# A conditioned short-convolution layer on one core: idle products in fewer instructions, adaLN's later pieces spread anew among the first weight loads, and first loads and splits in a fixed order

## The chip, the cores and the metric

The kernel runs on one core of a Trainium2 chip. The metric is device time in microseconds, the median of several runs; beside it stands one execution taken by the hardware profiler. The engines are TensorE (PE, its weight loads PEld), VectorE (DVE), ScalarE (ACT), GpSimd (POOL) and SyncE (SP), which issues nearly all DMAs. Each engine runs its instructions in the order in which the built program has them.

## What is computed

One layer: RMS norm, adaLN modulation by a conditioning vector, a gated short convolution, a gated residual, and a last RMS norm. T = 256 tokens, D = 2048, E = 4096, all in float32.

```
h = rmsnorm(x, norm_g)
shift, scale, gate = split(silu(c) @ ada_w + ada_b, 3)      # ada_w is 2048 x 6144
h = h * (1 + scale) + shift
b_gate, c_gate, v, g = split(h @ w_in, 4)                   # w_in is 2048 x 16384, 128 MB
u = causal_depthwise_conv(c_gate * v, conv_w)               # 3 taps
y = b_gate * u * silu(g)
x = x + gate * (y @ w_out)                                  # w_out is 4096 x 2048, 32 MB
return rmsnorm(x, final_g)
```

## The kernel before

**Products.** Features lie along partitions, tokens along the free axis; `hT` holds the modulated activations of 16 feature blocks k (0 to 15). To keep float32's accuracy each weight block is split into `hi`, a cast to fp32r by ACT (L338), and `lo`, the rest, by DVE (L339), and so is `hT`. Each block of 128x128 weights gives three products of 256 columns (L469): hi by hi, hi by lo, lo by hi.

**Two ways through w_in.** The products with a block k of `hT` can only be made when adaLN's shift and scale for k are known. `ada_w`'s columns for the first two k come first and on the path (16 rows of blocks `first_ada`, L211 to L219, summed by DVE at L365 and in part on PE by `sum0`). The others come in seven groups of two k, each in eight *pieces* of two DMAs of 256 KB (`ada_piece`, L425; tile `at`, four buffers) and two sums on DVE of each piece (L448, L450). Behind the last piece of a group four transposes on PE (`tp_g`, L457) and ACT, DVE give shift and scale. While these arrive, the first half of w_in's columns (four chunks `ch` of 512 columns in each of four quarters `q`) is worked in *passes*: `parts(chs, q, k0, k1, ...)` (L507) takes two chunks over the k at hand in one PSUM bank each (tile `mm_s`, three buffers), and its result goes to `acc` in SBUF: `keep` copies it out by ACT (L501) or adds it by DVE (L503). A later pass is opened either by ACT, which copies `acc` back into the bank (a seed, L517), or is added afterwards. The second half of the columns (tile `mm_b`) comes behind it with all k at once, and then the products with w_out (`mm_o`).

**The plan.** `plan()` (L55) works out with rough costs which pass covers which k, which pieces stand behind which load (`between`), and which passes are seeded. Credit grows by 1.5 a load of 1 MB, and each whole unit gives out one piece.

**Order.** The start, up to L404, is pinned in the order of the code. Behind that a scheduler orders each engine's instructions by data, buffers and priorities; adaLN's sums have a lower priority (`later(GIVE)`). `behind(ended)` holds the first loads, splits and sums behind the pinned part, but leaves their order among themselves to the scheduler.

**Names used below.** *Load n* is the n-th `raw_s` load of `parts` (L531; load 1 has 0.5 MB, the others 1 MB, three buffers). *Pieces p0 to p7* are the first group (k 2 and 3), p8 opens the next. *Chunk b0* is the bank that is filled from `raw0`, b1 that of load 1; load n from 2 on feeds b(2n-2) and b(2n-1). In the first passes a chunk is 24 products. With three banks, chunk b(n) needs the bank of b(n-3) copied out.

**Idle products.** `idle(n, where)` (L252) makes products of ones in the start, where PE would have nothing to do. Nothing reads them.

Of the kernel before, what the change touches and what calls it, by code (L numbers as in the profile page):

```python
# [49 lines left out]


SHARE = 1.5


def plan():  # L55
    steps, ready = [], [0.0] * ADA[0]
    done = {}
    pieces = [(sum(ADA[:g]), nk, i) for g, nk in enumerate(ADA) if g for i in range(4 * nk)]
    load, pe, dve, act = 0.0, 4.0, 0.0, 0.0
    burst = SLOT // P  # L60
    credit = -1.5

    def ada():
        nonlocal load, dve
        piece = pieces.pop(0)
        load = max(load, dve - AAHEAD) + ALOAD
        dve = max(dve, load + 2.0) + VPIECE
        if piece[2] == 4 * piece[1] - 1:
            ready.extend([dve + ALAG] * piece[1])
        return piece  # L70

    def products(n, need):

        nonlocal load, pe, dve, act, credit
        between = []
        load = max(load, pe - WAHEAD)
        pe = max(pe, need, load + min(n, burst) * LOAD + WLAG) + n * PRODUCTS
        for s0 in range(0, n, burst):
            sn = min(burst, n - s0)
            load += sn * LOAD  # L80
            act = max(act, load + 2.0) + sn * SBLOCK
            dve = max(dve, load + 2.0) + sn * VBLOCK
            credit += SHARE * sn / burst
            between.append([])
            while pieces and credit >= 1.0:
                credit -= 1.0
                between[-1].append(ada())
        return between

    order = [((ch, ch + 1), q) for ch in range(0, NCH, 2) for q in QUARTERS]  # L90
    new = [((0,), QUARTERS[0]), ((1,), QUARTERS[0])] + order[1:]
    while new or any(k < KT for k in done.values()):
        before = []
        hi = sum(r <= pe for r in ready)
        if new:
            p = new.pop(0)
            k0 = done[p] = 0
            if p not in order:
                del done[p]
                done[order[0]] = hi  # L100
        else:
            old = [p for p in order if done[p] < KT]
            p = old[0] if hi == KT else min(old, key=lambda p: done[p])
            k0 = done[p]
            while hi == k0:
                while len(ready) == hi:
                    before.append(ada())
                    credit -= 1.0
                pe = max(pe, ready[hi])
# [12 lines left out]
        steps.append((before, *p, k0, hi, hows, between))  # L122
        if p in order:
            done[p] = hi
    return steps


@with_exitstack
def short_conv_layer(ctx: ExitStack, tc: tile.TileContext, x, c, norm_g, ada_w, ada_b, w_in, conv_w, w_out, final_g, out):
    nc = tc.nc  # L130
# [22 lines left out]
    after = mybir.DependencyInfo(mybir.DependencyClass.NoSync, mybir.DependencyReason.DATA)  # L153
# [12 lines left out]
        ended.update(last)  # L166

    @contextmanager
    def behind(last):

        traced = nc.cur_bb.bb.instructions
        n = len(traced)
        yield
        for ins in list(traced[n:]):
            if ins.engine in last:
                tc.add_manual_dep(ins, last[ins.engine], after, reason="behind")

    @contextmanager
    def later(n):
# [10 lines left out]
    ended = {}  # L190
# [5 lines left out]
    rows2 = const.tile([96, P], F32, tag="rows2", name="rows2")  # L196
    HX = D // 2
    GIVE = 300
    IDLE = (20, 8, 20, 4, 4, 5, 11, 4)
    xt = [[slot([P, HX], f"x{t}{dh}") for dh in range(2)] for t in range(TT)]  # L200
    for t in range(TT):
        for dh in range(2):
# [8 lines left out]
    for n in range(KT // 4):  # L211
        at = wpool.tile([P, SLOT], F32, tag=("lo", "hi")[n % 2], name="at0", bufs=3)
        at = at.rearrange("p (k s f) -> p k s f", k=4, s=2)
        if n == 0:
            wpool.tile([P, 32], F32, tag="line3", name="line3", bufs=1)
        for j, kk in ((0, 2), (2, 2)) if n < 3 else ((0, 2), (2, 1), (3, 1)):
            for s in range(2):
                nc.sync.dma_start(at[:, j : j + kk, s, :], adas[:, 4 * n + j : 4 * n + j + kk, s, 0 : NK0 * P])
        first_ada.extend(at[:, i] for i in range(4))  # L219
# [31 lines left out]

    def idle(n, where):  # L252
        for _ in range(IDLE[n]):
            nc.tensor.matmul(where[:, 0, :], ones_r[:, 0:P], ones_r[:, T:], start=True, stop=True, skip_group_check=True)

    warm = const.tile([P, 1], F32, tag="warm", name="warm")
    silu = nc.scalar.activation(silu_c, turn(rows1, 64, 80, None), AF.Silu)
# [138 lines left out]
    w = CT * P  # L396
# [28 lines left out]
    def ada_piece(k0, nk, piece):  # L425
        w = nk * P
        kk = ASLOT // (2 * w)
        if piece == 0:
            sums[k0] = adap.tile([P, 2, 2 * P], F32, tag="gv", name="gv")
        gv = sums[k0][:, :, 0:w]  # L430
        j = piece * kk
        at = adap.tile([P, ASLOT], F32, tag="at", name="at", bufs=4)
        at4 = at.rearrange("p (k s f) -> p k s f", k=kk, s=2)
        for s in range(2):
            with behind(ended if first_loads else {}):
                nc.sync.dma_start(at4[:, :, s, :], adas[:, j : j + kk, s, k0 * P : k0 * P + w])
            first_loads[:] = first_loads[1:]
        with later(GIVE):
            ada_sums(j, kk, at4, gv)
        if j + kk == KT:  # L440
            ada_done(k0, nk, gv)

    def ada_sums(j, kk, at4, gv):
        for i in range(kk):
            c_k = silu_c[:, j + i : j + i + 1]
            if j + i == 0:
                with behind(ended):
                    nc.vector.tensor_scalar_mul(gv, at4[:, i], c_k)  # L448
            else:
                nc.vector.scalar_tensor_tensor(out=gv, in0=at4[:, i], scalar=c_k, in1=gv, op0=ALU.mult, op1=ALU.add)  # L450

    def ada_done(k0, nk, gv):

# [6 lines left out]
        modulate(k0, nk, (gs[:, 0:nk], gs[:, nk : 2 * nk]))  # L460

    opener = [None]
    first_loads = [None] * 16

    def product(dst, hi, lo, k, i, begins, left, ends):

# [35 lines left out]
        else:  # L502
            nc.vector.tensor_tensor(out=acc[ch, q], in0=bank, in1=acc[ch, q], op=ALU.add)  # L503

    first_pieces = [None] * 3

    def parts(chs, q, k0, k1, seeds, between):  # L507

# [17 lines left out]
        for s0, some in zip(range(k0, k1, step), between):  # L526
            sk = min(step, k1 - s0)
            n = sk * w
            raw = raw_tile("raw_s")
            with behind(ended if first_loads else {}):  # L530
                nc.sync.dma_start(  # L531
                    raw[:, :n].rearrange("p (k f) -> p k f", k=sk),
                    w_in[0, s0 * P : (s0 + sk) * P, col : col + w].rearrange("(k p) f -> p k f", p=P),
                )
            first_loads[:] = first_loads[1:]
            with behind(ended if first_pieces else {}):
                hi, lo = split(raw, n)
            first_pieces[:] = first_pieces[1:]
            for piece in some:
                ada_piece(*piece)  # L540
            for j, (bank, seed) in enumerate(zip(banks, seeds)):
# [241 lines left out]
```

## Time and profile before

| | |
|---|---|
| median of 3 runs | 918.99 us (917.21 to 919.25) |
| the profiled execution | 923.62 us, span 921.8 us |
| PE busy | 901.1 us, 98% |
| DVE, ACT busy | 626.7 us (68%), 467.0 us (51%) |
| mean granted clock of PE | 0.995 |
| DMA | 227.64 MB, mean 247 GB/s |

The span is the time from the first to the last instruction; the profiled execution's own time holds a little around it. A row of the timeline has the start and the length in us from the span's start, engine, line, operation and operands (written tile, arrow, read tiles), the count of merged instructions, and in brackets the idle time before it and who ended it. A list of waits has the total in us, how often, and the longest. `SPq` is SP's queue of DMA issues. The granted clock is PE's, 1.00 the full one.

### The profile page before, as it was taken

The page shows a single profiled execution, that of the slowest core. Times are in us where ns is not written, and L with a number is a line of the kernel's source. Part 1 is how long each engine was busy: PE and PEld are TensorE (multiplying, and loading weights), DVE is VectorE, ACT ScalarE, POOL GpSimd, SP SyncE. Part 2 cuts the span into 40 slices and gives each one's busy share as a digit, 9 for nine tenths or more (in the row PEclk, how much of TensorE's full clock was granted, in tenths as well). Part 3 has the DMA queues.
Part 4 walks back from the last instruction along what each step waited for, and adds up shares of the span by engine and source line. Part 5 has one row for each costly group of instructions (what it writes and reads, how often), then busy time and mean ns, then how long its engine had stood idle before and what let it go on. Part 6 is the DMA issues. An engine that isn't in the chain of part 4 may idle for free.

```text
span 921.8 us, 16333 instructions
## 1 busy us (share of the span) xinstructions
PE 901.1 (98%) x7091; PEld 867.5 (94%) x7091; DVE 626.7 (68%) x600; ACT 467.0 (51%) x445; POOL 2.3 (0%) x9
## 2 busy tenths in 40 slices
PE   7899999999999998999999999999999999999996
PEld 7899999999999998999999999999999988888885
DVE  5699998988887879976554554445554545545882
ACT  6579877656544648454334333443344433444333
POOL 1000000000000000000000000000000000000000
PEclk9999999999999999999999999999999999999999
DMA  9999999999888577777666665666666486566542
GB/s 305 373 362 362 331 376 367 338 339 357 306 302 319 184 254 278 240 227 223 191 185 196 200 197 183 193 201 202 183 185 197 140 347 228 187 202 204 184 137 91
DMA packets 146775, 227.64 MB, mean 247 GB/s; under 512 B 5456, under 2 KB 103808, under 8 KB 146320
## 3 DMA queue, kind: packets, MB, share of 16 engines
q1 hardware_dynamic: 146576, 226.51, 73.3%
q8 instruction: 55, 0.90, 0.4%
q14 instruction: 16, 0.13, 0.0%
q0 software_dynamic: 96, 0.08, 0.0%
q10 hardware_dynamic: 32, 0.01, 0.0%
HBM read 224.49 MB, written 2.10 MB: 246 GB/s over the span
## 4 chain that ended last, share of the span: by engine, by line
PE 83%; DMA 7%; DVE 5%; ACT 2%; issue 1%; SPq 0%; ACTq 0%; DVEq 0%
PE mm_b L469 38%; PE mm_s L469 26%; PE mm_o L681 6%; PE mm_o L680 6%; PE mm_o L679 6%; DMA at_g<-in_ada_w_dram 3%; DMA at<-in_ada_w_dram 2%; DVE lo L339 2%; DMA raw_s<-in_sc_w_in_dram 1%; DVE gacc L611 1%; ACT hi L338 1%; DMA x<-in_x_dram 1%; ACT mm_s L517 0%; ACT acc L501 0%; DVE acc L413 0%
## 5 line engine op out<-in xcount | busy, mean ns | idle before, releaser
L469 PE MATMUL mm_b<-hT,hi 128*128 128x256 f32 x2048 | 348.4, 276 | 0.0
L469 PE MATMUL mm_s<-hT,hi 128*128 128x256 f32 x2048 | 340.4, 278 | 6.4 <-ACT acc L501 3.1
L469 PEld LDWEIGHTS mm_s<-hT,hi 128*128 128x128 f32 x2048 | 302.0, 189 | 7.7 <-ACT acc L501 3.3
L469 PEld LDWEIGHTS mm_b<-hT,hi 128*128 128x128 f32 x2048 | 308.5, 188 | 0.0
L469 PE MATMUL mm_b<-hT,lo 128*128 128x256 f32 x1024 | 282.6, 276 | 0.0
L469 PE MATMUL mm_s<-hT,lo 128*128 128x256 f32 x1024 | 266.2, 278 | 0.9 <-DVE lo L339 0.8
L339 DVE TENSOR_TENSOR lo<-raw,hi 128x2048 fp32r<-128x2048 f32 x64 | 146.7, 2292 | 128.9 <-ACT hi L338 128.9
L338 ACT CAST hi<-raw 128x2048 fp32r<-128x2048 f32 x64 | 122.5, 1913 | 202.1 <-PE mm_b L469 150.8
L469 PEld LDWEIGHTS mm_b<-hT,lo 128*128 128x128 f32 x1024 | 192.2, 188 | 0.1
L469 PEld LDWEIGHTS mm_s<-hT,lo 128*128 128x128 f32 x1024 | 185.2, 189 | 1.5 <-DVE lo L339 1.5
L338 ACT CAST hi<-raw_s 128x2048 fp32r<-128x2048 f32 (+1 forms) x64 | 121.4, 1898 | 83.2 <-PE mm_s L469 69.2
L339 DVE TENSOR_TENSOR lo<-raw_s,hi 128x2048 fp32r<-128x2048 f32 (+1 forms) x64 | 145.5, 2273 | 22.5 <-ACT hi L338 19.0
L339 DVE TENSOR_TENSOR lo<-raw_o,hi 128x2048 fp32r<-128x2048 f32 x32 | 73.3, 2291 | 65.5 <-ACT hi L338 65.4
L338 ACT CAST hi<-raw_o 128x2048 fp32r<-128x2048 f32 x32 | 61.0, 1907 | 106.8 <-PE mm_o L681 84.0
L680 PE MATMUL mm_o<-lo,y 128*128 128x512 f32 x256 | 99.3, 389 | 0.0
L681 PE MATMUL mm_o<-hi,y 128*128 128x512 f32 x256 | 99.3, 389 | 0.0
L679 PE MATMUL mm_o<-hi,y 128*128 128x512 f32 x256 | 99.3, 389 | 0.0
L450 DVE SCALAR_TENSOR_TENSOR gv<-at,silu_c,gv 128x512 f32<-128x512 f32 x105 | 78.6, 749 | 2.6 <-DMA at<-in_ada_w_dram 0.8
L680 PEld LDWEIGHTS mm_o<-lo,y 128*128 128x128 f32 x256 | 48.0, 188 | 10.0
L679 PEld LDWEIGHTS mm_o<-hi,y 128*128 128x128 f32 x256 | 48.0, 188 | 10.0
L681 PEld LDWEIGHTS mm_o<-hi,y 128*128 128x128 f32 x256 | 48.0, 188 | 9.9
L501 ACT COPY acc<-mm_s 128x1024 f32<-128x1024 f32 x50 | 50.3, 1013 | 12.4 <-PE mm_s L469 12.4
(109 smaller groups left out, 388.4 us busy)
## 6 DMA issues: line engine op xcount, KB each, us to landing
raw<-in_sc_w_in_dram SPq DMA_DIRECT2D x64, 1024.0 KB, 5.6
raw_s<-in_sc_w_in_dram SPq DMA_DIRECT2D x63, 1024.0 KB, 7.4
raw_o<-in_sc_w_out_dram SPq DMA_DIRECT2D x32, 1024.0 KB, 5.2
at<-in_ada_w_dram SPq DMA_DIRECT2D x126, 256.0 KB, 7.3
at_g<-in_ada_w_dram SPq DMA_DIRECT2D x32, 512.0 KB, 7.3
x<-in_x_dram SPq DMA_DIRECT2D x4, 512.0 KB, 6.6
big<-in_x_dram SPq DMA_DIRECT2D x2, 1024.0 KB, 8.6
out_dram<-big SPq DMA_DIRECT2D x4, 512.0 KB, 2.9
```

What stands on the lines that cost most here:

```text
L338: nc.scalar.copy(hi[:, :n], raw[:, :n])
L339: nc.vector.tensor_tensor(out=lo[:, :n], in0=raw[:, :n], in1=hi[:, :n].bitcast(F32), op=ALU.subtract)
L450: nc.vector.scalar_tensor_tensor(out=gv, in0=at4[:, i], scalar=c_k, in1=gv, op0=ALU.mult, op1=ALU.add)
L469: mm = last_mm[0] = nc.tensor.matmul(dst, w, h[:, k], start=begins and left, stop=ends, skip_group_check=True)
L501: nc.scalar.copy(acc[ch, q], bank)
L611: nc.vector.scalar_tensor_tensor(out=ga, in0=at3[:, i, :], scalar=s, in1=ga, op0=ALU.mult, op1=ALU.add)
L679: nc.tensor.matmul(po, yh, hi[:, o], start=opens, stop=False, skip_group_check=True)
L680: nc.tensor.matmul(po, yh, lo[:, o], start=False, stop=False, skip_group_check=True)
L681: nc.tensor.matmul(po, yl, hi[:, o], start=False, stop=ct == NCT - 1, skip_group_check=True)
```

## The change

The kernel's products, results and sizes stay, apart from the idle products. Five edits go together:

1. The idle products come in fewer and wider instructions: 512 columns instead of 256, and for `idle(0)` to `idle(2)` in plain FP32 instead of fp32r (their ones read through `bitcast`).
2. The last four of the first adaLN columns come in eight single DMAs of 128 KB instead of two of 256 KB and four of 128.
3. `credit` starts at 0.0 and no longer at -1.5, by which `plan` hands out pieces one or two loads earlier, and comes to other passes from the ninth on. Behind it a list `PACE` spreads the pieces of the first ten loads anew: none behind the first three, then 2, 1, 2, 2, 2, 2, 2.
4. The first 28 DMAs of `parts` and `ada_piece` go through `load`, which holds each behind the one before on SP, in the order of the code.
5. The first ten splits are held in order on ACT and DVE (`advance=True`), and the sums of pieces behind the last split that the code has ahead of them.

```diff
+PACE = (0, 0, 0, 2, 1, 2, 2, 2, 2, 2)
...
-    credit = -1.5
+    credit = 0.0
...
+    blocks = [b for step in steps for b in step[-1]][: len(PACE)]
+    some = [piece for b in blocks for piece in b]
+    for b, n in zip(blocks, PACE):
+        b[:], some = some[:n], some[n:]
+    blocks[-1].extend(some)
     return steps
...
-    def behind(last):
+    def behind(last, advance=False):
...
+        if advance:
+            last.update((ins.engine, ins.name) for ins in list(traced[n:]) if ins.engine in last)
...
-    IDLE = (20, 8, 20, 4, 4, 5, 11, 4)
+    IDLE = (2, 1, 3, 2, 2, 3, 5, 2)
...
-        for j, kk in ((0, 2), (2, 2)) if n < 3 else ((0, 2), (2, 1), (3, 1)):
+        for j, kk in ((0, 2), (2, 2)) if n < 3 else ((0, 1), (1, 1), (2, 1), (3, 1)):
...
         for _ in range(IDLE[n]):
-            nc.tensor.matmul(where[:, 0, :], ones_r[:, 0:P], ones_r[:, T:], start=True, stop=True, skip_group_check=True)
+            both = ones_r.bitcast(F32) if n < 3 else ones_r
+            nc.tensor.matmul(where[:, 0:2, :], both[:, 0:P], both, start=True, stop=True, skip_group_check=True)
...
         for s in range(2):
-            with behind(ended if first_loads else {}):
-                nc.sync.dma_start(at4[:, :, s, :], adas[:, j : j + kk, s, k0 * P : k0 * P + w])
-            first_loads[:] = first_loads[1:]
+            load(at4[:, :, s, :], adas[:, j : j + kk, s, k0 * P : k0 * P + w])
...
-            if j + i == 0:
-                with behind(ended):
+            with behind(ended if first_pieces or j + i == 0 else {}):
+                if j + i == 0:
                     nc.vector.tensor_scalar_mul(gv, at4[:, i], c_k)
-            else:
-                nc.vector.scalar_tensor_tensor(out=gv, in0=at4[:, i], scalar=c_k, in1=gv, op0=ALU.mult, op1=ALU.add)
+                else:
+                    nc.vector.scalar_tensor_tensor(out=gv, in0=at4[:, i], scalar=c_k, in1=gv, op0=ALU.mult, op1=ALU.add)
...
-    first_loads = [None] * 16
+    first_loads = [None] * 28
+
+    def load(dst, src):
+
+        ins = nc.sync.dma_start(dst, src)
+        if first_loads:
+            sp = ins.ins.engine
+            tc.add_manual_dep(ins.ins, ended[sp], after, reason="in order")
+            ended[sp] = ins.ins.name
+            first_loads.pop()
...
-    first_pieces = [None] * 3
+    first_pieces = [None] * 10
...
-            with behind(ended if first_loads else {}):
-                nc.sync.dma_start(
...
-            first_loads[:] = first_loads[1:]
-            with behind(ended if first_pieces else {}):
+            load(
+                raw[:, :n].rearrange("p (k f) -> p k f", k=sk),
+                w_in[0, s0 * P : (s0 + sk) * P, col : col + w].rearrange("(k p) f -> p k f", p=P),
+            )
+            with behind(ended if first_pieces else {}, advance=True):
                 hi, lo = split(raw, n)
-            first_pieces[:] = first_pieces[1:]
+            del first_pieces[:1]
```

SP's DMAs behind the first two w_in loads, before. `raw_s_401` is load 2, `raw_s_467` load 3, `raw_s_537` load 4, `raw_s_602` load 5, `raw_s_672` load 6; `at_408`, `at_473`, `at_478`, `at_543`, `at_608` are p0 to p4.

```order
L531 DMA raw_s_401<-in_sc_w_in_dram 128x2x1024
L436 DMA at_408<-in_ada_w_dram 128x2x256 x2
L531 DMA raw_s_467<-in_sc_w_in_dram 128x2x1024
L436 DMA at_473<-in_ada_w_dram 128x2x256 x2
L436 DMA at_478<-in_ada_w_dram 128x2x256 x2
L436 DMA at_543<-in_ada_w_dram 128x2x256 x2
L531 DMA raw_s_537<-in_sc_w_in_dram 128x2x1024
L531 DMA raw_s_602<-in_sc_w_in_dram 128x2x1024
L436 DMA at_608<-in_ada_w_dram 128x2x256 x2
L531 DMA raw_s_672<-in_sc_w_in_dram 128x2x1024
```

The same place after: loads 2 to 6 are `raw_s_347`, `407`, `478`, `543`, `613`, and p0 to p4 `at_414`, `419`, `484`, `549`, `554`.

```order
L474 DMA raw_s_347<-in_sc_w_in_dram 128x2x1024
L474 DMA raw_s_407<-in_sc_w_in_dram 128x2x1024
L474 DMA at_414<-in_ada_w_dram 128x2x256 x2
L474 DMA at_419<-in_ada_w_dram 128x2x256 x2
L474 DMA raw_s_478<-in_sc_w_in_dram 128x2x1024
L474 DMA at_484<-in_ada_w_dram 128x2x256 x2
L474 DMA raw_s_543<-in_sc_w_in_dram 128x2x1024
L474 DMA at_549<-in_ada_w_dram 128x2x256 x2
L474 DMA at_554<-in_ada_w_dram 128x2x256 x2
L474 DMA raw_s_613<-in_sc_w_in_dram 128x2x1024
```

Load 3 moved ahead of p0, load 4 ahead of p2 and p3, and p3 and p4 now both stand ahead of load 6, where before load 6 stood behind p4 alone.

DVE at loads 4 to 6, before: `lo_540` is the low part of load 4, `lo_605` of load 5, `lo_675` of load 6; `gv_407` is the running sum of the first group.

```order
L450 SCALAR_TENSOR_TENSOR gv_407<-at_473,silu_c_133,gv_407 128x512
L339 TENSOR_TENSOR lo_540<-raw_s_537,hi_539 128x2048
L450 SCALAR_TENSOR_TENSOR gv_407<-at_478,silu_c_133,gv_407 128x512
L339 TENSOR_TENSOR lo_605<-raw_s_602,hi_604 128x2048
L450 SCALAR_TENSOR_TENSOR gv_407<-at_478,silu_c_133,gv_407 128x512
L450 SCALAR_TENSOR_TENSOR gv_407<-at_543,silu_c_133,gv_407 128x512 x2
L339 TENSOR_TENSOR lo_675<-raw_s_672,hi_674 128x2048
```

And after, where `lo_481` is the low part of load 4, `lo_546` of load 5, `lo_616` of load 6:

```order
L455 TENSOR_SCALAR gv_413<-at_414,silu_c_135 128x512
L348 TENSOR_TENSOR lo_481<-raw_s_478,hi_480 128x2048
L457 SCALAR_TENSOR_TENSOR gv_413<-at_414,silu_c_135,gv_413 128x512
L457 SCALAR_TENSOR_TENSOR gv_413<-at_419,silu_c_135,gv_413 128x512 x2
L348 TENSOR_TENSOR lo_546<-raw_s_543,hi_545 128x2048
L457 SCALAR_TENSOR_TENSOR gv_413<-at_484,silu_c_135,gv_413 128x512 x2
L457 SCALAR_TENSOR_TENSOR gv_413<-at_549,silu_c_135,gv_413 128x512 x2
L457 SCALAR_TENSOR_TENSOR gv_413<-at_554,silu_c_135,gv_413 128x512
L348 TENSOR_TENSOR lo_616<-raw_s_613,hi_615 128x2048
```

The second sum of p0 (`at_414`), which frees its buffer, moved behind the low part of load 4; before, p1's second sum (`at_473`, the first row there) stood ahead of that already.

ACT at the same place: the order of casts and copies is the same up to the copy-out of b2 (`acc02`) behind the cast of load 4; b3's copy-out (`acc12`) moved ahead of the cast of load 5. The last passes over the first half of w_in, as `plan` gives them (chunks, quarter, k from and to, loads), are before

```
(0,1) q0 10-16: 3   (2,3) q1 12-16: 2   (2,3) q2 14-16: 1   (2,3) q3 14-16: 1   (2,3) q0 6-16: 5
```

and after

```
(0,1) q0 14-16: 1   (2,3) q1 14-16: 1   (2,3) q2 6-16: 5   (2,3) q3 8-16: 4   (2,3) q0 12-16: 2
```

Behind the pass with q0 of channels 0 and 1 stands their mixing (`mixed`, L552: products, convolution and splits on DVE and ACT).

More of the change, by code (lines that the diff above doesn't have):

```diff
@@ L529, in parts @@
             raw = raw_tile("raw_s")
-            with behind(ended if first_loads else {}):
[L531 to L534, printed above, removed]
-            first_loads[:] = first_loads[1:]
-            with behind(ended if first_pieces else {}):
+            load(
[3 more added lines that the diff above has]
+            with behind(ended if first_pieces else {}, advance=True):
                 hi, lo = split(raw, n)
-            first_pieces[:] = first_pieces[1:]
+            del first_pieces[:1]
             for piece in some:
```

## The prediction

> **What bounds the kernel now.** I read the busy times by stage first, to see where TensorE (PE) waits at all; then the list of waits, for what ends these waits; then the timeline of the first 50 us. In the stage table the first pair of a row after the length is PE's busy time with its instructions.
>
> ```profile
> core 0: us, PE busy (x) PEld busy (x) DVE busy (x) ACT busy (x) POOL busy (x), PEclk, DMA share, GB/s
> 0.00:26.00 26.00, 19.76 (x142) 18.69 (x143) 13.73 (x26) 16.77 (x28) 2.33 (x9) 0.98 0.95 309
> 26.00:49.00 23.00, 19.94 (x151) 19.74 (x150) 16.18 (x17) 14.85 (x13) 0.00 (x0) 0.87 1.02 366
> 49.00:300.00 251.00, 250.57 (x2205) 250.14 (x2205) 223.22 (x250) 168.60 (x185) 0.00 (x0) 1.00 0.98 342
> 300.00:385.00 85.00, 81.17 (x701) 79.87 (x700) 75.91 (x91) 52.18 (x55) 0.00 (x0) 1.00 0.69 235
> 385.00:733.00 348.00, 348.00 (x3071) 347.90 (x3070) 192.41 (x148) 144.17 (x109) 0.00 (x0) 1.00 0.63 196
> 733.00:908.00 175.00, 175.00 (x804) 146.05 (x804) 102.67 (x66) 64.54 (x46) 0.00 (x0) 1.00 0.58 200
> ```
>
> PE is the bound, and the change leaves its products alone. From 385 to 908 us it never waits, and nothing there changes. What can be won lies in four stages: 6.24 us idle before 26, 3.06 in 26 to 49, 0.43 in 49 to 300, 3.83 in 300 to 385.
>
> ```profile
> PE mm_s L469 <- ACT acc L501: 3.1, 1, 3.1
> PE mm_s L469 <- DVE acc L503: 2.4, 1, 2.4
> PE mm_s L469 <- ACT mm_s L517: 0.9, 2, 0.5
> PE mm_s L469 <- DVE lo L339: 0.8, 2, 0.5
> ```
>
> The 3.1 us is one wait, and the timeline shows what stands behind it:
>
> ```profile
> 28.26 1.22 DVE L339 TENSOR_TENSOR lo<-raw_s,hi 128x1024 fp32r<-128x1024 f32 x1
> 31.19 3.15 SPq L531 DMA_DIRECT2D raw_s<-in_sc_w_in_dram  x2
> 31.65 2.29 DVE L339 TENSOR_TENSOR lo<-raw_s,hi 128x2048 fp32r<-128x2048 f32 x1
> 40.07 1.07 PE L469 MATMUL mm_s<-hT,lo 128*128 128x256 f32 x8
> 41.34 1.90 ACT L338 CAST hi<-raw_s 128x2048 fp32r<-128x2048 f32 x1 [4.70 <-DMA raw_s<-in_sc_w_in_dram]
> 43.14 1.01 ACT L501 COPY acc<-mm_s 128x1024 f32<-128x1024 f32 x1
> 44.20 2.61 PE L469 MATMUL mm_s<-hT,hi 128*128 128x256 f32 x16 [3.06 <-ACT acc L501]
> ```
>
> ScalarE (ACT) runs in order. The copy-out of bank b2 (43.14) could have run at 36, but it stands behind the cast of load 4, which waits 4.70 us for its data. PE's next chunk, b5, takes b2's bank. So a late load 4, needed by PE only at b6, stops PE at b5. The chain gives that load as
>
> ```profile
> 31.19 10.07 DMA raw_s<-in_sc_w_in_dram
> ```
>
> It was issued at 31.19 and landed at 41.26, behind the pieces p0 to p3 of adaLN (eight loads of 256 KB) in a busy queue. And the wait costs more than itself:
>
> ```profile
> 45.00:46.00 1.00, 1.00 (x10) 1.00 (x9) 1.00 (x2) 1.00 (x2) 0.00 (x0) 0.83 1.02 351
> 46.00:47.00 1.00, 1.00 (x6) 1.00 (x6) 1.00 (x2) 1.00 (x2) 0.00 (x0) 0.50 0.88 230
> 47.00:48.00 1.00, 1.00 (x7) 1.00 (x6) 1.00 (x1) 0.81 (x2) 0.00 (x0) 0.50 0.87 226
> 48.00:49.00 1.00, 1.00 (x7) 1.00 (x7) 1.00 (x2) 1.00 (x1) 0.00 (x0) 0.50 0.99 400
> 49.00:50.00 1.00, 1.00 (x10) 1.00 (x10) 0.93 (x3) 1.00 (x2) 0.00 (x0) 0.96 1.13 406
> ```
>
> The granted clock (first number after POOL) is halved from 45.9 to 49.3: 0.17+0.50+0.50+0.50+0.04 = 1.71 us of PE time lost. Together 4.77 us hang on load 4.
>
> **Part by part.** *Loads in fixed order.* On SP load 3 now stands ahead of p0, and only p0 and p1 stand ahead of load 4: four loads of 256 KB less.
>
> ```profile
> 17.00:18.00 1.00, 1.00 (x11) 1.00 (x11) 0.96 (x2) 1.00 (x3) 0.00 (x0) 1.00 1.10 349
> 35.00:36.00 1.00, 1.00 (x12) 1.00 (x11) 0.64 (x1) 1.00 (x2) 0.00 (x0) 1.00 1.11 377
> ```
>
> At 349 to 377 GB/s these 1.05 MB take 2.8 to 3.0 us. Load 4 lands at 41.26 - 2.9 = 38.4, if it is issued in time: its buffer is load 1's, free at 28.26+1.22 = 29.5, and its queue is then still full, so bandwidth decides. Cast 1.90, copy 1.01 with the same small steps (41.26 to 44.20 is 2.94): b5 can start at 41.35. PE ends b4 at 40.07+1.07 = 41.14, so 0.2 us remain of 3.06, too little to be read as idle by the clock. This gives -2.85 -1.71 = -4.55 us.
>
> *The price: p4 stands ahead of load 6.* `at` has four buffers, so p4 waits until both sums of p0 are done; p0's second sum now stands on VectorE (DVE) behind the low part of load 4. SP waits with everything behind p4. Chunks and loads there:
>
> ```profile
> 59.57 1.98 PE L469 MATMUL mm_s<-hT,hi 128*128 128x256 f32 x16
> 62.29 1.98 PE L469 MATMUL mm_s<-hT,hi 128*128 128x256 f32 x16
> 22.50 0.98 SPq L436 DMA_DIRECT2D at<-in_ada_w_dram  x2
> 33.86 0.74 DVE L450 SCALAR_TENSOR_TENSOR gv<-at,silu_c,gv 128x512 f32<-128x512 f32 x1
> raw<-in_sc_w_in_dram SPq DMA_DIRECT2D x64, 1024.0 KB, 5.6
> raw_s<-in_sc_w_in_dram SPq DMA_DIRECT2D x63, 1024.0 KB, 7.4
> ```
>
> Load 4's cast ends at 40.4, its low part at 42.7 (2.29), the sum at 43.4; p4's two loads 0.98, so load 6 is issued at 44.4 into a queue that has run empty. I take the 5.6 us of the last row but one (that queue is the less filled), not 7.4: landed 50.0, cast to 52.0, b6's bank copied out to 53.0. PE, a chunk every 2.72 us, wants that bank for b9 at 41.35+4x2.72 = 52.2: 0.8 us of new wait. With 7.4 it is 2.6, with less than 4.8 nothing. By the Trainium skill, "DMA: Bandwidth & Descriptors", section "Anatomy of one DMA", a DMA costs 2.0 us and its bytes at 436 GB/s; by that estimate load 6 takes 4.4 us, and the sum below would be 0.8 us better. The trace has no such load under 5.0 us, so I keep the rows.
>
> On DVE five sums (3.75) follow the low parts of loads 5 and 6; behind 52.0 that is low part 6 to 54.3, sums to 58.0, low part 7 to 60.3, three sums to 62.3, when p7 is complete. PE reaches the transposes of p7's result (`tp_g`, in chunk b12) at 53.0+3x2.72+0.9 = 62.1: 0.2 us. Behind that I take nothing: the stage table has PE waiting 0.43 us in the 251 from 49 on, and the loads behind load 7 are the same bytes in nearly the same order.
>
> *Eight single loads of 128 KB at the end of the first adaLN columns.* The chain into the first product is last landing, last sum, sum0, features:
>
> ```profile
> at<-in_ada_w_dram SPq DMA_DIRECT2D x1, 128.0 KB, 4.9
> 15.41 3.34 SPq L218 DMA_DIRECT2D at<-in_ada_w_dram  x5
> 23.48 0.75 DVE L365 SCALAR_TENSOR_TENSOR gv<-at,silu_c,gv 128x512 f32<-128x512 f32 x1 [0.41 <-DMA at<-in_ada_w_dram]
> 24.29 1.08 PE L351 MATMUL sum<-ones,gv 128*128 128x1 f32 x8 [0.41 <-DVE gv L365]
> ```
>
> SP's issues are 0.75 us apart here whatever their size (five in 3.34), since each waits for the landing of the eighth DMA before it. Two DMAs more put the last one's issue 1.5 us later. If its 4.9 us to landing is a latency, the first product is 1.5 late; if it is bandwidth (DMA share 1.10 in the row of 17 us, and the bytes are the same), nothing. I take 0.3, near the second end, for the queue and so for load 4 too.
>
> *Idle products.* In columns streamed, `idle(0..2)` pass 20, 8, 20 x 256 now; after, 2, 1, 3 x 512 in plain FP32, and the rest keep 1024, 1024, 1536, 2560, 1024 against 1024, 1024, 1280, 2816, 1024.
>
> ```profile
> 4.24 4.35 PE L254 MATMUL tp_x<-ones_r 128*128 128x256 f32 x20
> ```
>
> No FP32 product of that width is in the trace. At the rate of the others, 512 columns take 0.43 us cold (4.35/20x2), so `idle(0)` is over at 5.1; at four times that, 3.5 us, at 7.7. Neither end moves the first product, which waits for DMA until 24.29; but a colder PE could. I take nothing: a clock of 0.87 over 26 to 49 means 3.0 us lost, 1.3 more than the stretch above, so the first products run at half clock already; and b5 waits for load 4, not for them. The bound is +0.8 if the clock is lost for another 1.7 us of products ahead of b4's end.
>
> *The plan.* `credit` starts at 0 and no longer at -1.5, so passes move: one pass of columns 2 and 3 now takes k 0 to 4, the short passes of one load at the end stand elsewhere, and 15 adds of 1.22 us lie on DVE (12 before), with 27 instead of 34 seeding copies on ACT. PE's products stay. In 49 to 300 the table has DVE at 223 of 251 us: 3.7 more are covered. In 300 to 385 (75.9 of 85) they are not safely so:
>
> ```profile
> 339.35 0.75 DVE L611 SCALAR_TENSOR_TENSOR gacc<-at_g,silu_c,gacc 128x512 f32<-128x512 f32 x1 [5.64 <-DMA at_g<-in_ada_w_dram]
> 352.90 2.29 DVE L339 TENSOR_TENSOR lo<-raw_s,hi 128x2048 fp32r<-128x2048 f32 x1
> 356.37 1.22 DVE L503 TENSOR_TENSOR acc<-mm_s,acc 128x1024 f32<-128x1024 f32 x1
> ```
>
> DVE waits 5.64 us for a gate load, falls behind, and the add that frees a bank is late: the 2.4 us wait. Before, three passes of together four loads follow the mixing of channels 0 and 1 (the last two of one load each); after, one of one load and then one of five. The ends are -3.8 (all waits of this stage go) and +3.8 (they double). I take 0.
>
> Sum: -4.55 + 0.8 + 0.2 + 0.3 + 0 = -3.25 us. The profiled execution took 923.62 us (span 921.8), so 920.4 of its kind; the median of the runs shown is 918.99, 4.6 below it, and I carry the difference over: 915.7.
>
> **Rivals.** (1) *The wait only moves to load 6.* For it: SP is one queue, and p4 stands in it ahead of load 6. If load 6 takes the 10 us that load 4 took, it lands at 54.4, b9 waits 5.2 us and the clock falls again: -4.55+5.2+1.7+0.5 = +2.9, slower (921.9). It decides from a landing of 8.9 us on (7.2 if the clock falls as well); at 7.4 with the clock kept it gives 917.5. Against it: that queue has run empty.
> (2) *The late stage gets worse.* Place: DVE from 300 us; mechanism: an add behind mixing and gate sums, which wait for a landing. From +3.3 us there on the gain is gone; doubled waits give 919.5, three times the waits 923.3. For it: three adds more, and one-load passes still there. Against: PE's longest pass follows at once.
> (3) *The late stage gets better.* Its 3.8 us vanish: 911.9.
> (4) *The clock term isn't there.* The Trainium skill, "TensorE: Matmul & The Clock Gate", section "Part 1: The HAM clock gate", lets the clock fall after an idle window of about 3.4 us that runs freely. The row has a fall after only 3.06 us idle, so the trace does not bear that out as a rule for whole windows; but a fall lasts 3.4 us here too, and where its edges lie may differ from run to run. Where timed runs before the change kept the clock, the gain is 3.25-1.71 = 1.5: 917.5.
> (5) *The reorder does nothing*, as load 4 is late for another reason (its issue): then the 0.8, 0.2 and 0.3 stay: 920.3 at most, 919 if they hide in the old wait.
>
> **Numbers.** My forecast (-3.25, all within -1.9 to -5): 0.52. Rival 1: slower 0.04, half way 0.06. Rival 2: 0.10, half of it past the old time. Rival 3: 0.10. Rival 4: 0.10. Rival 5: 0.08. A change under 0.2% (1.8 us) can't be told from none in this kernel, so 917.15 to 920.8 is "the same". Faster: 0.52 + 0.10 + a third of rivals 1's half way and 4 (0.05) = 0.67. Slower: 0.04 + 0.05 + 0.01 = 0.10. The same: the rest, 0.23. The range runs from rival 3 (911.9) to the point where half of rival 2 and all of the slower ones are left out: 912 to 919.5. My forecast's own range is 914 to 917.1.
>
> **What would show it.** Right: no wait of PE over 1 us before 100 us; load 4's cast begins at 38 to 39, and the granted clock stays whole from 29 us on. Load 6's cast begins near 50, with a wait of under 1 us at the chunk b9. The first product starts at 26.2 to 26.6. PE's idle in 300 to 385, about 3.8. Wrong: the cast of load 4 still near 41; a wait of 3 us or more at b9 or at `tp_g`; a second half-clock stretch; a first product past 27; or more than 7 us idle behind 300.

## The result, and the profile after

The changed kernel is slower: 927.20 us median of six runs (926.47 to 930.7), against 919.52 us for the kernel before on the same chip (917.21 to 920.75). The ratio is 1.0093, 95% interval 1.0072 to 1.0113. The profiled execution took 930.7 us (span 928.6), against 923.62 (span 921.8).

The stage table of the changed kernel, its stages cut where its own work ends (columns as before):

```profile
core 0: us, PE busy (x) PEld busy (x) DVE busy (x) ACT busy (x) POOL busy (x), PEclk, DMA share, GB/s
26.00:49.00 23.00, 20.97 (x178) 20.23 (x177) 15.73 (x15) 14.42 (x12) 0.00 (x0) 1.00 0.90 309
49.00:60.00 11.00, 8.03 (x71) 7.83 (x70) 7.20 (x9) 4.72 (x4) 0.00 (x0) 1.00 0.89 315
60.00:90.00 30.00, 25.68 (x201) 25.11 (x201) 24.85 (x30) 19.31 (x24) 0.00 (x0) 0.89 1.02 367
90.00:120.00 30.00, 28.40 (x248) 28.00 (x247) 27.59 (x33) 26.31 (x31) 0.00 (x0) 1.00 1.01 345
120.00:300.00 180.00, 180.00 (x1589) 180.00 (x1588) 160.06 (x177) 100.54 (x112) 0.00 (x0) 1.00 0.95 333
300.00:392.00 92.00, 89.81 (x773) 89.30 (x773) 86.74 (x103) 56.77 (x58) 0.00 (x0) 0.98 0.76 260
```

The stretch from 26 to 49 us is better than it was: 2.0 us idle instead of 3.1, and the clock whole instead of 0.87. The loss stands where the prediction had put 1 us: 3.0 us idle in 49 to 60, and 4.3 us idle with a clock of 0.89 in 60 to 90. Another 1.6 us stand in 90 to 120; the late stage has 2.2 instead of 3.8. The list of waits names them:

```profile
PE mm_s L485 <- ACT acc L517: 4.2, 2, 3.0
PE mm_s L485 <- DVE hT L341: 2.8, 1, 2.8
PE mm_s L485 <- DVE acc L519: 2.2, 1, 2.2
PE mm_s L485 <- ACT mm_s L533: 1.5, 1, 1.5
PE mm_s L485 <- ACT hT L339: 1.5, 1, 1.5
```

(Lines of the changed kernel: L347 is the cast, L348 the low part, L455 and L457 the sums, L464 the transposes `tp_g`, L466 their reads, L339 to L341 the features, L474 every load, L485 the products, L517 and L519 copy-out and add, L533 the seed.)

The first wait of 3.0 us is that of load 6, in rows of the timeline from SP, DVE, ACT and PE (39.18 is the cast of load 4, 42.05 the first products of b5):

```profile
35.09 9.90 SPq L474 DMA_DIRECT2D at<-in_ada_w_dram  x4
39.18 1.91 ACT L347 CAST hi<-raw_s 128x2048 fp32r<-128x2048 f32 x1 [2.71 <-DMA raw_s<-in_sc_w_in_dram]
41.12 2.29 DVE L348 TENSOR_TENSOR lo<-raw_s,hi 128x2048 fp32r<-128x2048 f32 x1 [2.84 <-ACT hi L347]
42.05 2.10 PE L485 MATMUL mm_s<-hT,hi 128*128 128x256 f32 x16 [1.22 <-ACT acc L517]
43.33 2.32 DVE L457 SCALAR_TENSOR_TENSOR gv<-at,silu_c,gv 128x512 f32<-128x512 f32 x3
45.09 0.41 SPq L474 DMA_DIRECT2D raw_s<-in_sc_w_in_dram  x1
45.68 4.74 SPq L474 DMA_DIRECT2D at<-in_ada_w_dram  x4
53.33 1.90 ACT L347 CAST hi<-raw_s 128x2048 fp32r<-128x2048 f32 x1 [6.38 <-DMA raw_s<-in_sc_w_in_dram]
56.19 1.99 PE L485 MATMUL mm_s<-hT,hi 128*128 128x256 f32 x15 [2.98 <-ACT acc L517]
...
51.06 9.31 SPq L474 DMA_DIRECT2D at<-in_ada_w_dram  x4
60.46 0.93 SPq L474 DMA_DIRECT2D raw_s<-in_sc_w_in_dram  x2
```

DVE has nothing to do for 2.84 us; then it makes the low part of load 4, and only behind that p0's second sum. SP's four issues of p3 and p4 spread over 9.90 us, since p4 waits for p0's buffer. Load 6 is issued at 45.09, its cast begins at 53.33, and PE stops at b9. It goes on from there (last two rows): p8 needs p4's buffer, p4's sums stand behind the low part of the late load 6, SP's issues of p7 and p8 take 9.31 us, and loads 8 and 9 go out at 60.46.

The waits of 1.48 and 2.84 us are the first products with k 2:

```profile
65.76 0.60 PE L464 MATMUL tp_g<-ident,gv 128*128 128x128 f32 x4
68.75 1.92 ACT L347 CAST hi<-raw_s 128x2048 fp32r<-128x2048 f32 x1
70.56 0.27 ACT L466 ACTIVATE tp_g<-tp_g 128x128 f32<-128x128 f32 x1
72.56 0.26 ACT L466 ACTIVATE tp_g<-tp_g 128x128 f32<-128x128 f32 x1
74.42 1.91 ACT L347 CAST hi<-raw_s 128x2048 fp32r<-128x2048 f32 x1 [0.58 <-DMA raw_s<-in_sc_w_in_dram]
76.65 2.29 DVE L348 TENSOR_TENSOR lo<-raw_s,hi 128x2048 fp32r<-128x2048 f32 x1
77.17 1.09 ACT L339 ACTIVATE hT<-xs,shift,scale 128x256 fp32r<-128x256 f32 x2
77.83 0.62 PE L485 MATMUL mm_s<-hT,hi 128*128 128x256 f32 x3 [1.48 <-ACT hT L339]
80.82 0.75 DVE L341 TENSOR_TENSOR hT<-xs,hT 128x256 fp32r<-128x256 f32 x2
81.29 2.93 PE L485 MATMUL mm_s<-hT,hi 128*128 128x256 f32 x12 [2.84 <-DVE hT L341]
```

The transposes are done at 66.4. But on ACT their reads stand behind the cast of load 9 (68.75), and the features behind the cast of load 10, which waits for its data until 74.42; on DVE the features stand behind the low part of load 10. So a result that was there at 66.4 reaches PE at 77.8 and 81.3, and the clock falls:

```profile
79.00:80.00 1.00, 0.00 (x0) 0.00 (x0) 1.00 (x3) 0.00 (x0) 0.00 (x0) 0.52 1.01 406
82.00:83.00 1.00, 1.00 (x7) 1.00 (x7) 0.74 (x2) 0.46 (x1) 0.00 (x0) 0.50 1.09 351
85.00:86.00 1.00, 1.00 (x7) 1.00 (x6) 0.96 (x2) 0.00 (x0) 0.00 (x0) 0.57 1.00 396
```

From 81.29, when PE works again, to 85.1 half of its time is lost, 1.9 us. The features of k 2 and 3 thus cost 1.48 + 2.84 + 1.9 = 6.2 us, load 6 costs 3.0.

### The profile page after: what moved, and what is told of

Its sections match the earlier page's. It is cut to its first block, busy times and chain, and to the rows that moved or that the text cites. A ratio compares the mean times of both kernels' runs of the same rounds, so it can differ in the third digit from the quotient of the medians.

```text
span 928.6 us, 16211 instructions
## 1 busy us (share of the span) xinstructions
PE 901.8 (97%) x7041; PEld 862.6 (93%) x7041; DVE 629.7 (68%) x603; ACT 453.4 (49%) x431; POOL 2.3 (0%) x9
## 4 chain that ended last, share of the span: by engine, by line
PE 83%; DMA 8%; DVE 5%; issue 2%; ACT 2%; SPq 1%; ACTq 0%; DVEq 0%
PE mm_b L485 37%; PE mm_s L485 26%; PE mm_o L693 6%; PE mm_o L694 6%; PE mm_o L695 6%; DMA at<-in_ada_w_dram 3%; DMA raw_s<-in_sc_w_in_dram 3%; DMA at_g<-in_ada_w_dram 2%; DVE lo L348 2%; ACT hi L347 1%; DVE gacc L625 1%; DVE gv L457 1%; DVE acc L419 0%; DVE acc L422 0%; PE tp_g L464 0%
## 5 line engine op out<-in xcount | busy, mean ns | idle before, releaser
L485 PE MATMUL mm_s<-hT,hi 128*128 128x256 f32 x2048 | 342.1, 279 | 13.1 <-ACT acc L517 4.2
L485 PE MATMUL mm_b<-hT,hi 128*128 128x256 f32 x2048 | 348.4, 276 | 0.0
L485 PEld LDWEIGHTS mm_s<-hT,hi 128*128 128x128 f32 x2048 | 303.0, 190 | 15.8 <-ACT acc L517 4.8
L485 PEld LDWEIGHTS mm_b<-hT,hi 128*128 128x128 f32 x2048 | 308.2, 188 | 0.0
L485 PE MATMUL mm_b<-hT,lo 128*128 128x256 f32 x1024 | 282.6, 276 | 0.0
L485 PE MATMUL mm_s<-hT,lo 128*128 128x256 f32 x1024 | 263.4, 277 | 0.0
L348 DVE TENSOR_TENSOR lo<-raw,hi 128x2048 fp32r<-128x2048 f32 x64 | 146.7, 2292 | 133.6 <-ACT hi L347 133.6
L347 ACT CAST hi<-raw 128x2048 fp32r<-128x2048 f32 x64 | 122.4, 1913 | 199.9 <-PE mm_b L485 152.4
L485 PEld LDWEIGHTS mm_b<-hT,lo 128*128 128x128 f32 x1024 | 192.2, 188 | 0.1
L485 PEld LDWEIGHTS mm_s<-hT,lo 128*128 128x128 f32 x1024 | 184.1, 189 | 0.0
L347 ACT CAST hi<-raw_s 128x2048 fp32r<-128x2048 f32 (+1 forms) x64 | 121.5, 1899 | 109.8 <-PE mm_s L485 84.4
L348 DVE TENSOR_TENSOR lo<-raw_s,hi 128x2048 fp32r<-128x2048 f32 (+1 forms) x64 | 145.4, 2272 | 28.9 <-ACT hi L347 26.4
L348 DVE TENSOR_TENSOR lo<-raw_o,hi 128x2048 fp32r<-128x2048 f32 x32 | 73.3, 2291 | 64.3 <-ACT hi L347 64.3
L347 ACT CAST hi<-raw_o 128x2048 fp32r<-128x2048 f32 x32 | 61.0, 1907 | 106.8 <-PE mm_o L695 85.3
L457 DVE SCALAR_TENSOR_TENSOR gv<-at,silu_c,gv 128x512 f32<-128x512 f32 x105 | 78.5, 749 | 2.3 <-DMA at<-in_ada_w_dram 0.6
L517 ACT COPY acc<-mm_s 128x1024 f32<-128x1024 f32 x43 | 42.9, 1013 | 16.8 <-PE mm_s L485 16.8
```

The lines of the kernel that those rows point to most:

```text
L347: nc.scalar.copy(hi[:, :n], raw[:, :n])
L348: nc.vector.tensor_tensor(out=lo[:, :n], in0=raw[:, :n], in1=hi[:, :n].bitcast(F32), op=ALU.subtract)
L485: mm = last_mm[0] = nc.tensor.matmul(dst, w, h[:, k], start=begins and left, stop=ends, skip_group_check=True)
L517: nc.scalar.copy(acc[ch, q], bank)
```

## The experiments

Theory: the fixed order lets the sums of the first pieces stand behind low parts whose loads come later, so buffers of `at` come free late and SP stands still with load 6 (and 8 to 10) behind it; and the features of k 2 and 3 stand behind casts and low parts of these late loads. Rivals: the start (A), the changed passes (B), the order of loads itself (C, D). All times are medians; ratios are to the kernel before, run beside each.

| kernel | median us | ratio, 95% interval |
|---|---|---|
| changed | 927.20 | 1.0093 (1.0072 to 1.0113) |
| old start | 925.72 | 1.0090 (1.0070 to 1.0109) |
| old places of the pieces | 924.52 | 1.0077 (1.0058 to 1.0096) |
| old passes | 924.85 | 1.0073 (1.0058 to 1.0088) |
| no fixed order | 917.98 | 0.9999 (0.9983 to 1.0015) |
| only loads in fixed order | 920.98 | 1.0036 (1.0022 to 1.0049) |
| only casts, low parts, sums in fixed order | 922.07 | 1.0047 (1.0030 to 1.0063) |
| sums pinned | 920.86 | 1.0030 (1.0017 to 1.0042) |
| features first | 918.34 | 1.0005 (0.9992 to 1.0019) |
| both pins | 913.38 | 0.9955 (0.9938 to 0.9971) |
| both pins, old start | 913.01 | 0.9943 (0.9924 to 0.9961) |

**One edit undone at a time.**

*Old start.*

```diff
-    IDLE = (2, 1, 3, 2, 2, 3, 5, 2)
+    IDLE = (20, 8, 20, 4, 4, 5, 11, 4)
...
-        for j, kk in ((0, 2), (2, 2)) if n < 3 else ((0, 1), (1, 1), (2, 1), (3, 1)):
+        for j, kk in ((0, 2), (2, 2)) if n < 3 else ((0, 2), (2, 1), (3, 1)):
```

(with the 256-column product in `idle`.)

> The changed kernel with the start as it was: 256-column idle products in their old numbers and two single loads instead of eight at the end of the first adaLN columns. Theory (the 7.7 us lie between 40 and 95 us: load 6 late behind p4, then the features of k 2 and 3 late behind the casts of loads 9 and 10, then the halved clock): the time stays at 926 to 928, PE still waits about 3 us at load 6's chunk (53 us) and about 4 us at the first products of k 2 (76 to 81 us). Rival A (the start costs it: FP32 idle products or the eight loads): 919 to 921, and the first product is earlier by more than 1 us.

It stayed at 1.0090, with 2.48 and 2.39 us of waits at k 2. Its wait at load 6 was smaller than expected, 0.88 us, with 0.58 more behind load 7: load 6 was issued at 42.51 instead of 45.09 and its cast began at 50.67 instead of 53.33. The start doesn't carry the loss.

*Old places of the pieces.*

```diff
-PACE = (0, 0, 0, 2, 1, 2, 2, 2, 2, 2)
+PACE = (0, 0, 1, 2, 1, 2, 1, 2, 1, 2)
```

> The changed kernel with the old places of the pieces among the first loads (one piece ahead of load 3, then 2, 1, 2, 1, 2, 1, 2), all else as changed: fixed order, new passes, new start. Theory: the first sum of p0 then stands on DVE ahead of load 3's low part, about 7 us earlier than behind load 4's, p4 gets its buffer earlier and load 6 is issued near 38 instead of 45.1; the 2.98 us wait at 53 us goes, the features of k 2 and 3 come some us earlier and the 4.3 us at 76 to 81 with the halved clock shrink or go; load 4 is later by 0.5 MB, about 1.4 us: 918 to 922. Rival B (the changed passes cost it): 926 to 928.

A miss: 924.52. Load 6 was issued at 45.46, no earlier. p0's sums did move ahead, but now p5 stands ahead of load 6, and p5 needs the buffer of p1, whose second sum is again behind the low part of load 4. PE waited 1.04 us there, 2.19 at b5 and 0.90 + 1.69 at k 2 (in the profiled execution, which was the longest of the six, 928.18).

*Old passes.*

```diff
-    credit = 0.0
+    credit = -1.5
```

> The changed kernel with the old passes (credit starts at -1.5 again), the new places of the pieces, the fixed order and the new start. Theory: loads 1 to 9 and the pieces p0 to p8 stand as in the changed kernel, so the waits at 53 and 76 to 81 us stay; in the late stage 1.6 us are lost again: 926 to 929. Rival B (the changed passes cost it: the two-load pass of columns 2 and 3, three adds more): 916 to 920.

924.85, 1 us under what I expected, and its interval overlaps that of the changed kernel. The waits are in the same places: 2.05 at load 6, 3.10 and 2.63 us from 74.6 to 80.9; in the late stage, where I expected 1.6 us more, PE did not wait at all. Rival B falls as the cause; 0.2% for the passes can't be excluded.

*No fixed order.*

```diff
-    first_loads = [None] * 28
+    first_loads = [None] * 16
...
-    first_pieces = [None] * 10
+    first_pieces = [None] * 3
```

(and without `advance=True`, without the update of `ended` in `load`, and with only the first sum of a group held.)

> The changed kernel without the fixed order: 16 first loads held in order instead of 28, and the sums of the pieces free to run between the low parts as in the kernel before; new places of the pieces, new passes, new start. Theory: the sums of p0 run when its data is there, not behind load 4's low part, so p4's buffer is free earlier, load 6 is issued before 42 and the wait at 53 us goes; the features of k 2 and 3 follow earlier: 917 to 922. Rival B (the passes): 926 to 928. If only the wait at load 6 goes and the one at k 2 stays, 923 to 925.

917.98: the whole loss is gone, and no gain is left. SP doesn't stand still at p4, and load 6 goes out at 41.19:

```profile
34.05 3.85 SPq L474 DMA_DIRECT2D raw_s<-in_sc_w_in_dram  x2
41.19 0.37 SPq L474 DMA_DIRECT2D raw_s<-in_sc_w_in_dram  x1
```

PE waits neither at 53 nor at k 2. But it has a new wait: DVE takes p0's first sum ahead of the low part of load 2 and waits 5.19 us for p0's data.

```profile
PE mm_s L484 <- DVE lo L348: 2.7, 1, 2.7
```

So what is worth having is another order (both pins, below), not this one.

**Which half of the order.** *Only the loads* (28 loads in order, the other three lines as in the kernel without fixed order):

> The changed kernel with one half of the fixed order: the first 28 loads of SP stay in written order (p4 still ahead of load 6), the casts, low parts and sums are placed as in the kernel before. Theory (what costs is that the sums of p0 stand behind the low part of load 4, so p4's buffer comes free late and SP stands still): the first sum of p0 now stands ahead of the low part of load 2, p4 is issued before 41, load 6 lands before 51, no wait at 53 us and none over 1 us at k 2; instead DVE waits for p0 ahead of low part 2, which stops PE for 2 to 3.5 us near 35 (2.68 us in the run without any fixed order): 917 to 921. Rival C (the order of the loads itself, p4 ahead of load 6, costs it): 925 to 928.

920.98, at the upper end. p4 went out early enough that load 6 was issued at 40.77 instead of 45.09, with p4 still ahead of it; its cast began at 48.99. Rival C falls. PE waited 1.73 us for low part 2, a little less than said, and 1.77 at k 2, more than said.

*Only casts, low parts and sums* (`first_loads` 16 and no update in `load`):

> The changed kernel with the other half of the fixed order: casts, low parts and sums of the first ten parts stay in written order, of the loads only the first 16 (as before), so loads 4 to 7 stand ahead of p4 on SP. Theory: no wait at load 6's chunk (53 us), but p4 to p7 come later still, and the features of k 2 and 3 with them: PE waits 4 us or more at the first products of k 2: 923 to 929. Rival D (the fixed places of the sums are harmless, the fixed order of loads is what costs): 916 to 919.

922.07, a little under the range. No wait at load 6; 1.75 us at k 2, not 4. The biggest wait was one I had not named, 3.52 us at b5 with a clock of 0.93 in 26 to 49: without fixed loads p0 to p3 stand ahead of load 4 again, as in the kernel before. Rival D's range is missed too. The wait at load 6 is absent with either half alone, so it takes both.

**The two waits taken away by themselves.** *Sums pinned*: the next low part stands behind the sums written ahead of it.

```diff
-            with behind(ended if first_pieces or j + i == 0 else {}):
+            with behind(ended if first_pieces or j + i == 0 else {}, advance=bool(first_pieces)):
```

> The changed kernel with one more pin: the low part of each of the first loads also stands behind the sums of the pieces written ahead of it, so both sums of p0 and of p1 run between the low parts of loads 3 and 4 (where DVE has nothing from 37.9 to 41.1 us in the changed kernel). The order of the loads on SP is that of the changed kernel. Theory: p0's buffer is free near 39.5 instead of 44, p4 is issued near 39.5 and load 6 near 40.5, it lands before 49.5, the 2.98 us at 53 us go; the pieces behind come 4 us earlier, the features of k 2 and 3 too, and the 4.3 us at 76 to 81 with the halved clock go: 916 to 919. Rival C (p4 ahead of load 6 in SP's order costs it, whenever its buffer is free): 924 to 927.

The first half held to the letter. In the timeline of this kernel three sums fill DVE's gap ahead of low part 4, SP's four issues take 4.38 us instead of 9.90, and load 6 goes out at 39.52:

```profile
35.04 4.38 SPq L474 DMA_DIRECT2D at<-in_ada_w_dram  x4
37.76 2.33 DVE L457 SCALAR_TENSOR_TENSOR gv<-at,silu_c,gv 128x512 f32<-128x512 f32 x3
39.52 0.41 SPq L474 DMA_DIRECT2D raw_s<-in_sc_w_in_dram  x1
40.41 2.29 DVE L348 TENSOR_TENSOR lo<-raw_s,hi 128x2048 fp32r<-128x2048 f32 x1 [0.32 <-ACT hi L347]
```

The wait at 53 us is gone. The second half was wrong: the features did not follow. Shift and scale were ready 5 us earlier, but half of them still stood behind the low part of load 10, and 2.90 us of wait and a clock of 0.94 in 60 to 90 remained. 920.86, not 916 to 919. Rival C falls here too: p4 still stands ahead of load 6.

```profile
PE mm_s L485 <- DVE hT L341: 2.9, 1, 2.9
```

*Features first*: cast and low part of load 9 behind the reads of `tp_g` and shift and scale, those of load 10 behind the features; p4 is as late as in the changed kernel.

```diff
         for o in range(2 * nk):
             nc.scalar.activation(tp[:, o, :], tp[:, o, :], AF.Copy, accum_out=gs[:, o : o + 1])
+        if k0 == 2:
+            reads.update((ins.engine, ins.name) for ins in list(traced[n:]))
+        n = len(traced)
         modulate(k0, nk, (gs[:, 0:nk], gs[:, nk : 2 * nk]))
+        if k0 == 2:
+            reads.update((ins.engine, ins.name) for ins in list(traced[n : n + 3]))
+            made.update((ins.engine, ins.name) for ins in list(traced[n:]))
...
-                hi, lo = split(raw, n)
+                splits.append(raw)
+                with behind({9: reads, 10: made}.get(len(splits), {})):
+                    hi, lo = split(raw, n)
```

> The changed kernel with the features of k 2 and 3 moved ahead on ScalarE and VectorE: the four reads of tp_g and the shift and scale stand ahead of cast and low part of load 9, the features themselves ahead of cast and low part of load 10; nothing else is changed, p4 is as late as in the changed kernel. Theory: the 2.98 us at 53 us stay; the 1.48 and 2.84 us at 76 to 81 and the halved clock behind them (about 2 us) go: 919.5 to 923. Rival E (the features are late because the last piece is late, or another wait takes the place): 925 to 928.

918.34, better than the range. Rival E falls: the features now precede the cast of load 10 (the second of these rows):

```profile
72.93 1.09 ACT L339 ACTIVATE hT<-xs,shift,scale 128x256 fp32r<-128x256 f32 x2
...
74.83 1.91 ACT L347 CAST hi<-raw_s 128x2048 fp32r<-128x2048 f32 x1
```

```profile
PE mm_s L495 <- ACT acc L527: 4.0, 3, 2.2
PE mm_s L495 <- DVE hT L341: 0.8, 1, 0.8
```

The wait at load 6 is still there (2.22 us), the one at k 2 is 0.82 instead of 4.32, and no stage shows a lowered clock. A copy-out that now stands behind the cast of load 9 costs 1.20. That the kernel came out below the range goes with the waits at 103 and 329 us of the changed kernel, which are absent here; the pins move the order behind them too, and I did not separate that.

*Both pins.*

> The changed kernel with both pins: the low part of each of the first loads behind the sums written ahead of it (load 6 on time), and the reads of tp_g and the features of k 2 and 3 ahead of casts and low parts of loads 9 and 10 (features on time). Theory (the two waits add): no wait over 0.5 us at 53 us, at most 1 us at 72 to 78, clock whole: 3 us less than with the features alone (918.3): 914.5 to 917, and so faster than the kernel before. Rival F (what the pins move in the order behind 90 us decides as much as these two waits): 918 to 921, with new waits of together over 2 us behind 85 us.

913.38: faster than the kernel before by 0.45% (interval 0.29 to 0.62), and 1.1 us under the expected range. Of the waits of `mm_s` these are left:

```profile
PE mm_s L495 <- ACT hi L347: 1.1, 1, 1.1
PE mm_s L495 <- ACT acc L527: 0.3, 1, 0.3
```

and from 49 us on PE is never idle and at full clock:

```profile
49.00:60.00 11.00, 11.00 (x95) 11.00 (x95) 10.44 (x11) 7.88 (x8) 0.00 (x0) 1.00 1.05 386
60.00:90.00 30.00, 30.00 (x266) 30.00 (x265) 26.63 (x31) 26.30 (x34) 0.00 (x0) 1.00 1.06 379
300.00:381.00 81.00, 81.00 (x713) 80.83 (x712) 77.65 (x93) 50.34 (x51) 0.00 (x0) 1.00 0.76 262
```

The four kernels make a square: 1.0093 with neither pin, 1.0030 and 1.0005 with one, 0.9955 with both. Alone the pins give 0.63 and 0.88%, together 1.38%, near the sum of 1.51. Rival F falls.

*Both pins and the old start.*

> The same two pins, and the start as it was before the change (256-column idle products, two single loads instead of eight). Theory (the start is worth little): within 2 us of the kernel with both pins and the new start, 914 to 918. Rival A (the new start costs or gains something that the waits behind it covered): more than 2 us from it.

913.01, within 0.4 us; the best of all, though its interval overlaps that of the kernel with the new start.

**Both kernels profiled once more.**

> The kernel before once more, with a profile. The first profiled execution took 923.62 us, 4.6 to 5.5 more than the median of the timed runs. Theory (halved-clock stretches are part of that difference and not of every execution): the wait for load 4 near 41 us is there again at 2.5 to 3.5 us, but if this execution is near the median (917 to 920), the granted clock is whole from 30 us on. Rival G (the stretch at 46 us belongs to the wait): it is there again, and an execution near the median saves its time elsewhere.

This execution of the kernel before took 916.39 us. The wait for load 4 is there, 2.79 us, and the clock does not fall behind it:

```profile
42.51 2.10 PE L469 MATMUL mm_s<-hT,hi 128*128 128x256 f32 x16 [2.79 <-ACT acc L501]
```

```profile
46.00:47.00 1.00, 1.00 (x11) 1.00 (x10) 1.00 (x2) 0.65 (x2) 0.00 (x0) 1.00 0.97 373
300.00:385.00 85.00, 84.15 (x735) 83.44 (x734) 79.28 (x96) 55.05 (x57) 0.00 (x0) 1.00 0.72 247
```

The late stage has 0.85 us of waits instead of 3.83. Rival G falls in this execution.

> The changed kernel once more, with a profile. Its first profiled execution took 930.7 us, 3.5 more than the median. Theory: the waits at load 6's chunk (2 to 3 us at 52 to 56) and at the first products of k 2 (together 3.5 to 5 us at 74 to 81) are there again; what makes an execution faster is the start (waits for loads 1 and 4 ahead of 42 us) or where the clock falls: 925 to 930. Rival: one of the waits is absent, or the late one (2.19 us at 329 us) is, and the time is below 924.

928.98 us: 3.00 us at load 6, 1.70 and 2.83 at k 2, 1.52 at 106; the late wait of 2.2 us is absent in this execution, without the time below 924 that the rival gave for that, and the clock fell at 58 and again at 82.

## Why the prediction was wrong, point by point

- **Load 4: the mechanism was right.** Its cast began at 39.18, 0.2 us past "38 to 39"; b5 started at 42.05, predicted 41.35. The wait shrank from 3.06 to 1.22 us here, to 0.24 in the second execution, and to 0.27 to 0.62 in the three kernels with pins and the new start.
- **The clock term was not a sure one.** That was rival 4, given 0.10. In the second execution of the kernel before the clock stays whole behind nearly the same wait; there the gain in reach was 2.8 us, not 4.55. How often it falls at this place is not recorded. The 63 timed executions of the kernel before that stand beside the experiments have mean granted clocks from 0.993 to 0.999 (0.995 in the profiled one with the fall, 0.998 in the one without); the 17 at 0.995 or less have a median of 918.1 us, the 11 at 0.998 or more 917.0.
- **Carrying the 4.6 us over was a mistaken step.** I took the distance from profiled execution to median as a constant. The 7.2 us between the two profiled executions of the kernel before hold a fallen clock (twice: 25 to 29 and 46 to 49), and 3.0 us of late waits: terms of my sum that not every execution has. The second one, 916.39, lies below every median of this kernel (917.54 to 919.52), so a median execution may have part of them. Rivals 2 and 3, on the late stage, rested on the same 3.83 us.
- **Load 6: the right place, a wrong size.** Issue predicted 44.4, measured 45.09. Landing I took 5.6 us later, "into a queue that has run empty"; it took about 8.2. The queue had run empty (DMA share 0.04 from 44 to 45 us). p4's two DMAs stand ahead and four piece DMAs follow within 5 us; why the load took so long is not shown. With sums pinned it took 8.4 from an issue at 39.52, so the row of `raw_s` (7.4) was nearer than that of `raw`. The wait was 2.98, not 0.8; 7.4 would have given 2.6. By the Trainium skill, "DMA: Bandwidth & Descriptors", section "Anatomy of one DMA — SWDGE (gpsimd) path", an estimate for this load is 4.4 us: that fit is for one DMA issued through GpSimd, and here, for a load that SP issues among others, the measurement decides against it.
- **"Behind that I take nothing" is the step that failed most.** It put the way of p7's result to PE, behind the transposes, at nothing. I followed the group's result only to the transposes on PE (predicted 62.1, run at 65.76 without a wait) and stopped. Behind the transposes lie four reads on ACT, three small operations on DVE, and features on both, each in an engine's queue with casts and low parts that wait for loads. That cost 6.2 us. The argument, "the same bytes in nearly the same order", holds for the bytes; but p8 stops SP as p4 does, and I had followed that only for p4. No rival of mine named it: rival 1 has its mechanism, a piece that stops SP, at load 6 alone. (In the sum up to there, three sums of 0.75 behind 60.3 end at 62.5, not 62.3; the 0.2 us of that term would have been 0.4.)
- **The start: right that it matters little.** The first product came at 25.30, earlier than before (26.23 and 25.60) and not later; load 1 came later (cast at 27.74; 26.71 and 26.46 before), and PE waited 0.72 us for it. The two kernels with the old start stand within 0.12% of their partners. `idle(0)` ran to 7.75, the end that I had worked out for four times the rate.
- **The plan: right within what was measured.** A wait for an add stands in one of the two executions of the changed kernel (2.2 us) and not in the other; the old passes gave 0.2%, inside the intervals.

## What to carry to other kernels

When an order is pinned, follow each late result to the last instruction that uses it, on every engine that it passes, and ask what stands ahead of it there that waits for a transfer: a queue in order turns a late load into a wait for work that doesn't need the load. A buffer that a transfer waits for is set free by an instruction whose place in another engine's queue is as much part of the DMA order as the DMA's own. Take two or three profiled executions before summing terms: a stretch of halved clock or a late stage's wait that only one of them shows is no sure term of the median.

## What the hardware showed that I had not expected

The clock falls after waits much shorter than I had thought, and not always. Behind a wait of 2.19 us from 328.80 it was halved:

```profile
332.00:333.00 1.00, 1.00 (x6) 1.00 (x6) 1.00 (x1) 1.00 (x2) 0.00 (x0) 0.50 0.26 94
```

(from 331.2 to 335.0 us), while the wait of 2.98 us at load 6 left it whole in one execution of the changed kernel, and the same wait of 3.00 in the next was followed by 0.50 from 58 us on, a microsecond after PE had resumed:

```profile
58.00:59.00 1.00, 1.00 (x11) 1.00 (x10) 0.96 (x2) 0.00 (x0) 0.00 (x0) 1.00 0.38 123
58.00:59.00 1.00, 1.00 (x7) 1.00 (x7) 0.96 (x3) 0.00 (x0) 0.00 (x0) 0.50 0.68 239
```

The Trainium skill, "TensorE: Matmul & The Clock Gate", section "Part 1: The HAM clock gate", lets it fall after at least one idle window of about 3.4 us that runs freely. That the same wait can do both agrees with windows that run freely; that 2.19 us were enough does not agree with a whole idle window.
